# A two-layer network by nested fast products: x's transposes in one burst, stores and weight loads queued behind them, and another order in the first pair

## The chip, the cores and the metric

The kernel runs on one core of one Trainium2 chip. The metric is the device time of one execution in microseconds (us), as a median of several runs. TensorE (PE) multiplies matrices into PSUM banks. VectorE (DVE) and ScalarE (ACT) read those banks and do elementwise work. GpSimd (POOL) and SyncE (SP) mostly issue transfers here. All transfers run on the core's 16 DMA engines. A transfer is issued on the queue of SP, ACT or POOL, and the instructions of one queue are taken in order.

## The reference

`x` is 8 x 1024 x 1024, `w1` 1024 x 4096 and `w2` 4096 x 1024, all float32.

```python
h = x @ w1
h = 0.5 * h * (1 + np.tanh(np.sqrt(2 / np.pi) * (h + 0.044715 * h ** 3)))
return (h @ w2).astype(np.float32)
```

## The kernel before

**Tiling.** The 8192 rows of `x` are taken in eight superblocks of 1024 rows, numbered 0 to 7. In each, both matrix products are split into 2 x 2 blocks, named "11", "12", "21" and "22", and computed by a scheme of seven products instead of eight. Products 1, 2, 3 and 4 use a plain block on the weights' side or on the rows' side, and products 5, 6 and 7 use sums of blocks on both. Superblocks 0 and 1 use the scheme once (`matmul1`, `matmul2_made`). Superblocks 2 to 7 use it twice, one inside the other. They load all sums of the weights from DRAM, where superblocks 0 and 1 have stored them.

**The first layer, in superblocks 0 and 1.** `matmul1` walks over pairs of column chunks (j = 0 to 7). A pair has seven products of two halves each, and 4 matmuls of 128 x 512 for each half (L501), so 56 matmuls. Product 4 of a pair runs at the start of the next pair, after the next pair's product 1. The weights come in groups of four chunks, two pairs to a group (`MadeQuad`). A group holds the four raw blocks of `w1` and the sums 5, 6, 7 and 4 of them. In superblock 1 the raw blocks are loaded from DRAM (L202), the sums are made on VectorE, and each is stored for later superblocks (L247). `inner_sums(m)` makes four further sums of operand m, which only the later superblocks need, in four short VectorE instructions, and stores them (L260). The rows' side is `XOps`: x's four transposed blocks and the sums x5 = 21 + 22, x7 = 11 - 21, x6 = 22 - x7, x3 = x6 - 12.

**The second layer, in superblock 0.** `matmul2_made` runs products 1, 2, 5, 6, 3, 7 and 4 in this order. A plain one has four rows q of 16 matmuls (L1184), so `(6, 3)` is the last row of product 6. Product 3 is "deep": it is itself computed by seven smaller products (L1129, class `Inner`) and has seven steps. After each row or step, `run` carries out the jobs that the table `FILL` lists under that place. Their letters mean: `g`, sums of the activated rows; `wMq`, part q of the sum M of `w2`'s blocks, for product M; `pMN`, the split N of operand M of `w2`, a sum that later superblocks need (it is made on VectorE and stored in `in_d`, L1012); `a`, sums for the deep product; `x`, a sum of x's blocks; `q`, a sum of `w1`'s first group; `i`, inner sums of that group. Product 4 reads all four parts `w40` to `w43`, and its row q goes on in the bank that product 7's row q has used, after VectorE's addition has read that bank.

**x for the next superblock.** After row `(5, 0)` POOL issues eight transfers that cast x's rows to float16 into the DRAM tile `xb` (L476). After row `(6, 3)` SP issues 16 transposing transfers (L165), four for each block, in the order 22, 21, 12, 11. Ahead of them on SP stand twelve stores (`keep`) of `w2`'s blocks 21, 12 and 22, four each. After row `(7, 0)` the first group of `w1` for superblock 1 is loaded on ACT's queue.

**Buffers.** The pool `up` has 24 buffers of 4 KiB per partition (tiles named `u`). They hold `w2`'s blocks and the sums written over them, splits, x's blocks, x's sums and groups of `w1`. The pool `mp` (tiles `mu`) has two; the splits 7 and 4 of operands 1, 2 and 3 are made there. A buffer is free again when its last reader is done, and a store counts as a reader until it has landed. The deep product 3 reads the splits of operand 3 from these tiles.

**Order.** A planner orders each engine's instructions when the kernel is built. What is pinned (`keep_in_program_order`, `load_in_order`, `tt(..., pin=True)`) stays behind the instruction traced before it on its engine. The loads of `MadeQuad` and the stores of the splits are not pinned; all VectorE work named here is.

Of the kernel before, what the change touches and what calls it, by code (L numbers as in the profile page):

```python
# [23 lines left out]
SUMS = tuple(W_SUM)  # L24
# [13 lines left out]
""".split()  # L38
BEGIN = {"m37": (0,), "m24": (1,2), "m34": (3, 4)}
SPLIT_IN_M1 = ()  # L40


def slots(table):
# [6 lines left out]
    ;50:w60 w61;51:w62 w63;52:g30 g31;53:g32 g33  # L50
    ;60:p35 p36;61:a35 p37;62:a37 p34;63:a36
    ;31:w70;32:a33;33:w71;34:w72;35:w73;36:p25;37:p26
    ;70:p27 p24;71:w40 w41;72:w42 w43;73:x5;40:q5;41:x7 x6;42:x3 q6 q7 q4
    ;43:i2 i7 i3 i1 i5""".replace("\n    ", "")),
    slots("""10:g60 w50;11:g61 w51;12:g62 w52;13:g63 w53
    ;20:g50 p55;21:g51 p56;22:g52 p57;23:g53 p54
    ;50:w60 w61;51:w62 w63;52:g30 g31;53:g32 g33
# [18 lines left out]
def kernel(  # L76
# [7 lines left out]
    nc = tc.nc  # L84
# [107 lines left out]
    class MadeQuad:  # L192


        def __init__(self, q, first, store):
            self.q, self.first, self.store = q, first, store
            self.raw = {b: unit(2 * KH, 2 * P) for b in BLOCKS}
            self.ops = {m: self.raw[b] for m, b in W_TERM.items()}
            if not first:
                queue = nc.sync if q else nc.scalar  # L200
                for b in ("12", "11", "22", "21") if q else ("12", "11", "21", "22"):
                    queue.dma_start(out=halves(self.raw[b]), in_=w1_at(q, term.get(b, b)))  # L202

        def load(self):
# [330 lines left out]
    def matmul1(xs, sb, quads, start=None):  # L535
        g = g_tiles()

        def gelu(b, c, src):
            gelu_into(g[b][:, c, :], src)

        def ahead(j):

            if j // 2 == NI // QC - 1:
                return ()
            q, second = divmod(j, 2)
            if not second:
                quad = MadeQuad(q + 1, sb == 0, sb == 1)
                quads.append(quad)
                if sb == 0:
                    quad.load()  # L550
                    quads[q].keep_raw()
            quad = quads[q + 1]
            if sb == 0:
                return [lambda m=m: quad.sum(m, pin=True) for m in SUMS] if second else ()
            jobs = [lambda m=m: quad.sum(m, pin=True) for m in ((7, 4) if second else (5, 6))]
            inner = ((2, 7, 5, 3) if second else (1,)) if q == 0 else ((2, 7, 3) if second else ())
            return jobs + [lambda m=m: quad.inner_sums(m) for m in inner]

        nxt = {}
        splits = []  # L560
        late = None
        for j in range(NI // 2):
            cs = (2 * j, 2 * j + 1)
            end = j == NI // 2 - 1
            source = quads[j // 2]
            if start is not None and j == 0:
                start.pair(gelu)
                ahead(j)
                continue
            jobs = list(ahead(j))  # L570
            banks_a = [psum(), psum()]
            a = [temp(), temp()]

            def one(h):
                product(banks_a[h], source, xs, 1, cs[h], True)
                act_copy(a[h], banks_a[h])

            swap = sb == 1 and j == 0
            for h in range(0 if swap else 2):
                one(h)  # L580
            banks_c, p5, t = [], [], [temp(), temp()]

            def five(h):
                if len(p5) == h:
                    banks_c.append(psum())
                    p5.append(temp())
                    product(banks_c[h], source, xs, 5, cs[h], True)
                    act_copy(p5[h], banks_c[h])

            def six(h):  # L590
                product(banks_a[h], source, xs, 6, cs[h], False)
                act_copy(t[h], banks_a[h])

            def seven(h):
                product(banks_a[h], source, xs, 7, cs[h], False)
                tt(p5[h], banks_a[h], p5[h], SUB, True)

            def three(h):
                product(banks_c[h], source, xs, 3, cs[h], False)

            banks_b = [psum(), psum()]
            for h in range(2):
                if late is not None:
                    gelu("12", late[1][h], late[3][h])
                if late is not None:
                    product(late[2][h], late[0], xs, 4, late[1][h], False)
                    gelu("21", late[1][h], late[2][h])
                elif swap:
                    five(h)
            for h in range(2):  # L610
                product(banks_b[h], source, xs, 2, cs[h], True)
            for h in range(2 if swap else 0):
                one(h)
            for h in range(2):
                add(a[h], banks_b[h])
            difference(g, j - 1)
            half = (len(jobs) + 1) // 2
            if start is not None and j == 1:
                rest = jobs[2:]
                half, jobs = 2, [lambda m=m: quads[0].sum(m, (2, 2), True) for m in (7, 4)] + jobs[:2]  # L620
            elif start is not None and j == 2:
                half, jobs = 2, rest
            if sb == 1:
                half = 3 if j % 2 else 0
                if j != 4:
                    jobs += splits
                    splits = []
            for job in jobs[:half]:
                job()
            if end:  # L630
                six(0)
                gelu("11", cs[0], a[0])
                six(1)
                gelu("11", cs[1], a[1])
                for h in range(2):
                    five(h)
                for h in range(2):
                    seven(h)
                    gelu("22", cs[h], p5[h])
                    three(h)  # L640
                for h in range(2):
                    product(banks_a[h], source, xs, 4, cs[h], False)
                    gelu("21", cs[h], banks_a[h])
                for h in range(2):
                    tt(t[h], t[h], banks_c[h], SUB, True)
                    gelu("12", cs[h], t[h])
            else:
                first = j == 0
                five(0)
                if not first:  # L650
                    gelu("11", cs[0], a[0])
                five(1)
                six(0)
                if not first:
                    gelu("11", cs[1], a[1])
                six(1)
                for h in range(2 if first else 0):
                    gelu("11", cs[h], a[h])
                three(0)
                three(1)  # L660
                seven(0)
                seven(1)
                for h in range(2):
                    gelu("22", cs[h], p5[h])
                for h in range(2):
                    tt(t[h], t[h], banks_c[h], SUB, True)
                late = (source, cs, banks_a, t)
            for job in jobs[half:]:
                job()
            if sb == 1 and j < 2 * len(SPLIT_IN_M1):  # L670
                splits = split_in_m1(SPLIT_IN_M1[j // 2], j % 2)
            if sb == 1 and j > 4:
                for q in {5: (0,), 6: (1,), 7: (2, 3)}[j]:
                    nxt["xb"] = x_cast_paced(sb + 1, g["11"][:, 2 * j + 1, :], 2 * q, nxt.get("xb"))
        difference(g, NI // 2 - 1)
        return g, nxt.get("xb")
# [175 lines left out]
    def matmul2_made(sb, g, keep_w1, xb):  # L852
# [111 lines left out]
        for m, name, first in (  # L964
# [10 lines left out]
            for q in range(NQ):  # L975
# [4 lines left out]
                post(m, q, bank)  # L980
                if (m, q) == (5, 0) and sb == 0:
                    xb = x_cast(sb + 1, nc.gpsimd.tensor_copy(out=pace, in_=p5[0][:, :2]))
                if (m, q) == ((5, 0) if sb else (6, NQ - 1)):
                    xs = XOps(x_transpose(xb, load_in_order))
                if (m, q) == (6, 0):
                    keep("22")
                if (m, q) == (7, 0) and sb == 0:
                    quad = MadeQuad(0, False, True)
# [10 lines left out]
    def split_jobs(m, pieces, t):  # L999

        def operand(v, h):
            if isinstance(v, int):
                return t[v][:, h * QC:(h + 1) * QC, :]
            k, b = int(v[0]) - 1, int(v[1]) - 1
            return chunks(pieces()[2 * k + h])[:, b]

        def make(n):
            u, op, v = W_SUM[n]
            t[n] = (mp.tile([P, NI // 2, OH // 2], DT, name="mu") if n in (7, 4) and m != 4 else unit(NI // 2, OH // 2))
            for h in range(2):  # L1010
                tt(t[n][:, h * QC:(h + 1) * QC, :], operand(u, h), operand(v, h), op, True)
            nc.gpsimd.dma_start(out=in_d[m][:, SUMS.index(n)], in_=t[n])  # L1012

        return [lambda n=n: make(n) for n in SUMS]

# [307 lines left out]
```

## Time and profile before

| | |
|---|---|
| median of 3 runs | 1463.32 us (1462.68 to 1464.65) |
| the profiled execution | 1467.66 us, its span 1465.8 us |
| TensorE busy | 1450.3 us, 99% of the span |
| VectorE busy | 1207.9 us, 82% |
| ScalarE busy | 711.7 us, 49% |
| GpSimd busy | 588.2 us, 40% |
| moved by DMA | 460.13 MB, mean 314 GB/s |
| mean granted TensorE clock | 0.997 |

A line of the timeline gives the start and the length of a merged run of instructions, the engine, the line of the kernel, the operation, what it writes and reads, how many there are, and in brackets how long the engine had been idle before and what released it. `SPq` and `ACTq` are transfers issued on the queues of SP and ACT. A line of the windows gives, for one stretch, its length, each engine's busy time with its count of instructions (PE, PEld, DVE, ACT, POOL), the granted TensorE clock, the busy share of the DMA engines and the GB/s that they moved. A group of transfers shows how long their issue took (least, median, most, in ns), when the first and the last were issued, and the time from issue to landing.

### The profile page before, as it was taken

Reading aid. Unit: us, or ns where it says so; the run is one execution under the profiler, and the core shown is the slowest. Engines: PE = TensorE matmul, PEld = TensorE weight load, DVE = VectorE, ACT = ScalarE, POOL = GpSimd, SP = SyncE. Lnnn points to the kernel's source line nnn. Section 1 sums busy time; section 2 is a strip of 40 time slices with the busy share of each in tenths; the row PEclk is TensorE's granted clock in tenths of the full one; section 3 lists DMA queues with packets and bytes.
Section 4 is the critical chain, followed back from the end, with each engine's and each line's share of the span. In section 5 each row is a group of like instructions: output and inputs, shape, how many; then the busy total and the mean of one; then the engine's idle time right before and its main releaser. Section 6 shows DMA issues by size and latency. Waiting matters only on the chain.

```text
span 1465.8 us, 28916 instructions
## 1 busy us (share of the span) xinstructions
PE 1450.3 (99%) x10731; PEld 1049.1 (72%) x10731; DVE 1207.9 (82%) x2019; ACT 711.7 (49%) x1460; POOL 588.2 (40%) x606
## 2 busy tenths in 40 slices
PE   9999988999999999999999999999999999999998
PEld 5444633444477888778887788777887778877887
DVE  5657748758688898889898898988989889898887
ACT  5665115641158621785228841388224872268621
POOL 1442213222359500793018820388005960068400
PEclk9999999999999999999999999999999999999999
DMA  9999999798799999999999999999999999987594
GB/s 327 336 350 380 330 270 331 256 328 239 275 395 249 287 379 365 330 254 317 352 351 331 241 361 337 366 299 224 386 356 353 264 266 370 354 337 234 207 402 168
DMA packets 199117, 460.13 MB, mean 314 GB/s; under 512 B 75201, under 2 KB 80321, under 8 KB 198081
## 3 DMA queue, kind: packets, MB, share of 16 engines
q1 hardware_dynamic: 176672, 371.25, 74.3%
q0 software_dynamic: 21344, 84.95, 17.9%
q10 hardware_dynamic: 960, 2.10, 0.6%
q8 instruction: 84, 1.38, 0.4%
q14 instruction: 57, 0.46, 0.1%
HBM read 370.15 MB, written 102.76 MB: 323 GB/s over the span
## 4 chain that ended last, share of the span: by engine, by line
PE 85%; DMA 8%; issue 4%; POOL 2%; ACT 1%; SPq 0%; DVE 0%; POOLq 0%; DVEq 0%
PE ps L1129 36%; PE ps L721 23%; PE ps L501 19%; PE ps L1184 6%; DMA gc<-in_w_dram 4%; DMA u<-in_w_dram 2%; DMA w_d<-u 1%; PE ps L434 1%; POOL u L171 1%; DMA xb<-in_x_dram 1%; ACT u L168 0%; POOL in_d L1012 0%; POOL out_dram L838 0%; DMA u<-in_x_dram 0%; PE ps L411 0%
## 5 line engine op out<-in xcount | busy, mean ns | idle before, releaser
L168 ACT COPY tmp<-ps 128x512 f32<-128x512 f32 (+1 forms) x528 | 263.7, 539 | 239.8 <-PE ps L501 155.4
L501 PE MATMUL ps<-u 128*128 128x512 f16 x1472 | 347.1, 382 | 8.7 <-DVE u L141 4.8
L1129 PE MATMUL ps<-u,gc 128*128 128x256 f16 x2704 | 308.6, 273 | 0.0
L1129 PEld LDWEIGHTS <-gc 128*128 128x128 f16 x2816 | 275.5, 98 | 31.9
L141 DVE TENSOR_TENSOR tmp<-tmp,ps 128x256 f32<-128x256 f32 (+1 forms) x368 | 197.1, 543 | 73.6 <-PE ps L721 30.7
L501 PEld LDWEIGHTS <-u 128*128 128x128 f16 x1472 | 144.9, 98 | 153.3 <-issue 9.7
L141 DVE TENSOR_TENSOR u<-u 128x2048 f16<-128x2048 f16 (+3 forms) x292 | 221.2, 801 | 38.4 <-PE ps L1129 14.1
L721 PEld LDWEIGHTS <-u 128*128 128x128 f16 x2096 | 205.0, 98 | 57.3
L850 POOL DMA_DIRECT2D out_dram<-u x50 | 36.7, 735 | 500.6 <-DVE u L141 478.1
L1129 PE MATMUL ps<-u,g 128*128 128x256 f16 x2000 | 234.8, 273 | 0.0
L1129 PEld LDWEIGHTS <-g 128*128 128x128 f16 x2112 | 206.6, 98 | 24.3
L721 PE MATMUL ps<-u 128*128 128x256 f16 x1372 | 221.0, 273 | 0.0
L514 ACT ACTIVATE g<-tmp 128x512 f16<-128x512 f32 x282 | 173.9, 639 | 57.7 <-DVE tmp L141 57.1
L168 ACT COPY ps<-ps 128x256 f32<-128x256 f32 (+1 forms) x208 | 95.2, 458 | 219.5 <-PE ps L1129 219.3
L141 DVE TENSOR_TENSOR ps<-tmp,ps 128x256 f32<-128x256 f32 x444 | 181.4, 426 | 17.1 <-PE ps L721 9.4
L168 ACT COPY u<-ps 128x512 f32<-128x512 f32 (+1 forms) x114 | 66.2, 587 | 179.5 <-PE ps L1129 146.0
L141 DVE TENSOR_TENSOR u<-u,ps 128x512 f32<-128x512 f32 x174 | 118.4, 683 | 40.0 <-ACT u L168 20.0
L514 ACT ACTIVATE g<-ps 128x512 f16<-128x512 f32 x230 | 137.9, 600 | 24.7 <-PE ps L721 14.9
L773 POOL TENSOR_TENSOR tmp<-tmp 128x512 f32<-128x512 f32 x96 | 122.2, 1276 | 41.4 <-DVE tmp L141 31.8
L1184 PE MATMUL ps<-u,g 128*128 128x512 f16 x640 | 138.8, 379 | 0.0
L141 DVE TENSOR_TENSOR tmp<-ps,tmp 128x512 f32<-128x512 f32 x126 | 86.8, 690 | 55.2 <-PE ps L501 46.2
L1184 PEld LDWEIGHTS <-g 128*128 128x128 f16 x640 | 62.6, 98 | 75.3
(72 smaller groups left out, 1571.9 us busy)
## 6 DMA issues: line engine op xcount, KB each, us to landing
u<-w_d SPq DMA_DIRECT2D x343, 512.0 KB, 9.1
u<-in_d SPq DMA_DIRECT2D x162, 512.0 KB, 9.2
out_dram<-u POOLq DMA_DIRECT2D x50, 512.0 KB, 7.6
gc<-in_w_dram SPq DMA_DIRECT2D x48, 512.0 KB, 6.5
g<-w_d SPq DMA_DIRECT2D x45, 512.0 KB, 8.0
w_d<-u POOLq DMA_DIRECT2D x40, 512.0 KB, 6.5
w_d<-u SPq DMA_DIRECT2D x32, 512.0 KB, 9.5
xb<-in_x_dram POOLq DMA_DIRECT2D x56, 256.0 KB, 6.9
```

The lines of the kernel that those rows point to most:

```text
L141: i = nc.vector.tensor_tensor(out=out, in0=in0, in1=in1, op=op)
L168: tc.keep_in_program_order(nc.scalar.copy(out=out, in_=in_))
L171: pool_last[0] = nc.gpsimd.tensor_copy(out=out, in_=in_)
L434: tc.keep_in_program_order(nc.tensor.matmul(bank[:, cols], lhsT=w[:, k, :], rhs=self.xs.blocks[f"{a}{r}"][:, k, cols], start=r == 1 and k ...
L501: tc.keep_in_program_order(nc.tensor.matmul(bank, lhsT=w, rhs=x, start=first and k == 0, stop=k == n - 1, skip_group_check=not first,))
L514: gelu_last[0] = nc.scalar.activation(out=out, in_=src, func=GELU, scale=scale)
L721: tc.keep_in_program_order(nc.tensor.matmul(out, lhsT=w, rhs=x, start=first and k == 0, stop=k == 1, skip_group_check=not first,))
L773: tc.keep_in_program_order(nc.gpsimd.tensor_tensor(out=t, in0=t, in1=temp("p", m), op=ADD))
L850: return nc.gpsimd.dma_start(out=rows, in_=src, **kw)
L1129: tc.keep_in_program_order(nc.tensor.matmul(bank[:, i * OH // 2:(i + 1) * OH // 2], lhsT=t[:, c, i * P:(i + 1) * P], rhs=self.weights(j, c ...
L1184: tc.keep_in_program_order(nc.tensor.matmul(pair(bank), lhsT=a[:, c, :], rhs=chunks(pieces[c // QC])[:, :, c % QC, :], start=(first and c ...
```

## The change

- In superblock 0, the 16 transposes of x for superblock 1 are issued after row `(6, 0)` instead of `(6, 3)`. The four stores of `w2`'s block 22 are issued after `(6, 3)` instead of `(6, 0)`, so behind the transposes.
- The four stores of the splits of operand 3 go to SP's queue instead of POOL's. They are made at the same places as before, which lie behind the transposes in program order.
- The four loads of `w1`'s first group go to SP's queue instead of ACT's, in the order 11, 21, 12, 22 instead of 12, 11, 21, 22.
- The first pair of superblock 1 runs its products in the order 1, 2, 5 like every other pair; before, it ran 5, 2, 1.
- In `FILL[0]`, x7 and x6 come one or two rows earlier, and `q5` moves behind x3. Of five sets of inner sums at `(4, 3)` only set 2 stays. Sets 7 and 3 are made in the first pair, behind its two additions, and sets 1 and 5 in the third (`FIRST_INNER`).

```diff
+FIRST_INNER = {0: (7, 3), 2: (1, 5)}
...
-    ;70:p27 p24;71:w40 w41;72:w42 w43;73:x5;40:q5;41:x7 x6;42:x3 q6 q7 q4
-    ;43:i2 i7 i3 i1 i5""".replace("\n    ", "")),
+    ;70:p27 p24;71:w40 w41;72:w42 w43;73:x5;40:x7;41:x6;42:x3 q5 q6 q7 q4
+    ;43:i2""".replace("\n    ", "")),
...
-                queue = nc.sync if q else nc.scalar
-                for b in ("12", "11", "22", "21") if q else ("12", "11", "21", "22"):
+                queue = nc.sync
+                for b in ("12", "11", "22", "21") if q else ("11", "21", "12", "22"):
...
-            swap = sb == 1 and j == 0
-            for h in range(0 if swap else 2):
+            for h in range(2):
                 one(h)
...
-                elif swap:
-                    five(h)
             for h in range(2):
                 product(banks_b[h], source, xs, 2, cs[h], True)
-            for h in range(2 if swap else 0):
-                one(h)
             for h in range(2):
                 add(a[h], banks_b[h])
...
+            for m in FIRST_INNER.get(j, ()) if sb == 1 else ():
+                quads[0].inner_sums(m)
...
-                if (m, q) == ((5, 0) if sb else (6, NQ - 1)):
+                if (m, q) == ((5, 0) if sb else (6, 0)):
                     xs = XOps(x_transpose(xb, load_in_order))
-                if (m, q) == (6, 0):
+                if (m, q) == (6, 3):
                     keep("22")
...
-            nc.gpsimd.dma_start(out=in_d[m][:, SUMS.index(n)], in_=t[n])
+            (nc.sync if m == 3 else nc.gpsimd).dma_start(out=in_d[m][:, SUMS.index(n)], in_=t[n])
```

## The prediction

> **What bounds the kernel now.** I read the page first, then TensorE's timeline, then every engine's timeline around its gaps, then groups of the DMA queues.
>
> ```profile
> PE 1450.3 (99%) x10731; PEld 1049.1 (72%) x10731; DVE 1207.9 (82%) x2019; ACT 711.7 (49%) x1460; POOL 588.2 (40%) x606
> ```
>
> TensorE is the bound; only its idle and its slow time can be won. Its timeline from 100 to 320 us has two gaps, both between superblocks 0 and 1:
>
> ```profile
> 179.34 27.79 PE L1184 MATMUL ps<-u,g 128*128 128x512 f16 x128
> 211.92 14.70 PE L501 MATMUL ps<-u 128*128 128x512 f16 x56 [4.79 <-DVE u L141]
> 230.56 86.43 PE L501 MATMUL ps<-u 128*128 128x512 f16 x392 [3.94 <-DVE tmp L141]
> ```
>
> Products 7 and 4 end at 207.1; the first pair waits 4.79 us for VectorE, the second 3.94. Windows of 2 us (sixth figure: granted clock) show what follows each gap:
>
> ```profile
> 210.00:212.00 2.00, 0.08 (x1) 0.08 (x2) 1.23 (x1) 0.00 (x0) 0.00 (x0) 0.52 1.11 250
> 212.00:214.00 2.00, 2.00 (x5) 0.64 (x6) 0.00 (x0) 0.15 (x1) 1.23 (x2) 0.50 1.10 315
> 216.00:218.00 2.00, 2.00 (x8) 0.78 (x7) 1.97 (x3) 0.18 (x1) 0.00 (x0) 0.78 1.06 412
> 232.00:234.00 2.00, 2.00 (x6) 0.68 (x5) 1.97 (x3) 2.00 (x5) 0.28 (x1) 0.51 1.00 381
> ```
>
> Half clock costs the first pair 14.70 - 56 x 0.216 = 2.6 us, and the second (3.4 us at half, to 234.9) 1.7. In all 4.8 + 2.6 + 3.9 + 1.7 = 13.0 us can be won. The timeline of all engines says why:
>
> ```profile
> 177.93 27.15 SPq L165 DMA_TRANSPOSE u<-xb  x14
> 200.22 1.23 DVE L141 TENSOR_TENSOR u<-u 128x2048 f16<-128x2048 f16 x1 [6.18 <-DMA u<-xb]
> 201.11 3.66 ACTq L202 DMA_DIRECT2D u<-w_d  x4
> 210.64 1.23 DVE L141 TENSOR_TENSOR u<-u 128x2048 f16<-128x2048 f16 x1 [9.19 <-DMA u<-w_d]
> 214.23 14.48 DVE L141 TENSOR_TENSOR u<-u 128x2048 f16<-128x2048 f16 x26 [2.36 <-DMA u<-xb]
> ```
>
> x5 waits for transposes, q5 for w1's first loads, and 26 sums in a row then hold back the first pair's additions.
>
> **The change part by part.** I follow its order with the times of this trace.
>
> 1. The burst. It needs x's cast rows, and block 22 (transposed first) needs the last ones. The eight casts:
>
> ```profile
> L476 POOL DMA_DIRECT2D xb<-in_x_dram x8: 493/496/527, 149.7 to 153.1; - x8
> DMA to landing us min/median/max: 7.7/10.8/14.0
> ```
>
> The last lands at 153.1 + 14.0 = 167.1. Transposes start at 170.3 today, so passing four stores on SP wins 3.2 us of start, no more; nothing touches the casts. Their pace then is SP's. Today's 16 took 34.8 us, among POOL's stores; eight in a quieter stretch of superblock 2 show:
>
> ```profile
> L165 SPq DMA_TRANSPOSE u<-xb x8: 1122/1252/1622, 649.5 to 659.1; - x8
> DMA to landing us min/median/max: 2.7/3.4/6.3
> ```
>
> (659.1 - 649.5) / 7 = 1.37 us each, so 16 take 21.9: issued by 189.0. I take this row since POOL's four p3 stores leave the stretch, and its later ones wait for VectorE (step 2); the ends are 16 x 1.25 = 20.0 and today's 34.8. The Trainium skill (DMA: Bandwidth & Descriptors, Latency and other measured facts) gives a DMA transpose 261 GB/s: 2.1 MB would take an estimated 8 us, the stores behind would land by about 180, step 2 would cost nothing, and the sum would be the first rival's. The trace's 131 KB per 1.37 us is 96 GB/s and disagrees.
>
> 2. What stands behind the burst: p35, p36, p37, p34, w2's four blocks, w1's four loads. POOL loses four issues of 0.53 us and ACT the 3.66 us of loads at 201.1; neither is on the path (product 4's copies had until 211.9), so 0. The second group's loads now stand behind all this on SP (today issued from 205 to 215), but its sums run at 232. What counts is that landing frees buffers. In deep product 3 the 24 u buffers are all taken: w2's blocks with the sums written over them 16, product 6's halves 2, p35 and p36 2, x's blocks 4. So p25 and p26 need buffers that a store releases, p27 and p24 the two mu buffers of p37 and p34. Today these stores landed at 169 to 176 and VectorE ran:
>
> ```profile
> 179.18 1.28 DVE L141 TENSOR_TENSOR u<-u 128x1024 f16<-128x1024 f16 x2
> 183.67 2.49 DVE L141 TENSOR_TENSOR mu<-u 128x1024 f16<-128x1024 f16 x4
> 187.06 2.35 DVE L141 TENSOR_TENSOR u<-u 128x2048 f16<-128x2048 f16 x2
> 190.51 2.35 DVE L141 TENSOR_TENSOR u<-u 128x2048 f16<-128x2048 f16 x2
> ```
>
> Now p35's store is issued at 189 and lands some 4 us on (2.7 to 6.3 above), at 193; the others 1.45 us apart (512 KB at the 364 GB/s of 226 to 231). VectorE stands from 179.2 to 193. Behind p25 it has, at this trace's starts, put 0.6, p26 1.2, product 7's first addition 0.6, p27 1.2, p24 1.2, the second addition 0.6, w40 1.1; with p25's 1.2 that is 7.7, so w40 is ready at 200.7, w41 at 201.9, and behind one more addition w42 at 203.6 and w43 at 204.8. Product 4 could start at 193.2 (179.34 + 64 x 0.217) but reads all four. TensorE so idles 7.5 us, and runs some 6 us at half clock as after 211.92: row 0's 16 matmuls end at about 207.1, the other 48 (10.4 us) at 217.5. That is 10.4 us later than today. Cover against this would be the stores ahead of the burst; bound from below: 0.
>
> 3. Order 1, 2, 5 and the weights' new queue and order. The first pair needs x's blocks 11 and 12 (landed by 193) and w1's 11, then 21; x5 and q5 3.5 us later, q6 5.2 us later. VectorE is through with the last addition at 205.4, x5, x7, x6, x3 (4 x 1.14) by 210. From 190 the DMA engines owe 12 transfers on SP (17.4 us) and about 11 us of POOL's stores: w1's 22 lands near 219 at 360 GB/s. It is needed by 217.5 + 5.2 - 1.1 = 221.6. Cover 2.6 us: cost 0. By the 234 GB/s of 187 to 207 the debt takes 45 us, 22 lands at 235 and costs 13; I take the fast end, since those windows held transposes and this stretch holds none.
>
> 4. The four inner sums moved. Ahead of the additions VectorE now has one set (1.4 us) for five. Sums 7 and 3 (2.8 us) fall between the additions and product 7's subtraction, which TensorE reaches 10.4 us into the pair: hidden, as are 1 and 5 in the third pair, by the same 10 us. Both second losses (3.9 and 1.7) go.
>
> Sum: the first pair runs from 217.5 for 56 x 0.216 = 12.1, to 229.6. Today the second is free at 230.56 and loses 1.7 more: 232.3. Gain 2.7, of which I leave 0.5 for VectorE's additions: 2.2 us. The profiled execution took 1467.66 (span 1465.8), 4.3 above the median; 2.2 off the median of 1463.32 is 1461.1. By step 1's ends: a burst over at 187 gives 1459, one over at 202 1474; eight transposes among stores (341.8 to 352.2) took 1.48 each, 191 and 1463, so the slow end is left outside the main case.
>
> **Rivals.** *No stall* (the p3 stores pass the burst, not being pinned as the transposes are, so the change does less than it says): product 4 ends at 207.1, w1's 11 lands at 211, as today's q5 at 210.64 shows for the same bytes, and the pair ends at 223.1: 9.2 us won, 1454, or 1457 with 2.6 of half clock. For it: p35 is written by 160, well before 167.1. Against it: p37 and p34 come later, and the burst stands first in program order. *Weights late*, the side that is slower: they stand last, behind eight stores that ACT's queue let them pass. For it, 234 GB/s; against it, 371 from 218 to 226. Each us beyond 221.6 costs one; it decides against the change from 221.6 + 2.2 + 2.9 = 226.7 on; half way between the two landings, 227, it costs 5.4: 1466.5. The Trainium skill (the same page, Issuing engines are not separate DMA queues) says that all issuers share the same 16 engines, so a new queue takes no bytes off; the share near 1.0 in every window agrees. *A buffer of w2's fourth block for p25*: four stores on, 5.8 us later, 1467.
>
> **How the numbers follow.** Main case 0.48, no stall 0.21, weights late 0.21, fourth block's buffer 0.10. About 0.2% (2.9 us) is what this measurement can tell from no change. The main case, 1461.1 with its own range 1456 to 1465, splits 0.16 faster, 0.31 same, 0.01 slower; with the first rival faster, the last two slower: faster 0.37, same 0.31, slower 0.32. The range reaches to 1453 (no stall) and 1469 (weights at 229.5).
>
> **What would show it.** Right: transposes from 167 to 190 on SP; VectorE idle some 14 us from 179 with a DMA named; TensorE idle before product 4, none at 207 and 227. Wrong: VectorE running on at 179 (no stall); transposes beginning later than 170 or among stores; TensorE waiting at the first pair (weights).

## The result and the profile after

The change takes 1466.89 us as a median of 22 runs (1464.70 to 1469.30); the kernel before, run beside it, takes 1463.82 (22 runs, 1460.14 to 1468.27). The ratio is 1.0023 with a 95% interval of 1.0016 to 1.0029: some 3 us slower, where the forecast was 2 us faster. A second comparison later gave 1466.10 against 1464.08, ratio 1.0008 (0.9996 to 1.0020), so the loss is small, but it is no gain. The profiled execution of the change took 1467.82 us, its span is 1466.0. That of before took 1467.66. By these two profiles alone the change would do nothing, and this turns out to be the heart of the case.

The page after, the line of the engines:

```profile
PE 1449.4 (99%) x10731; PEld 1049.3 (72%) x10731; DVE 1207.9 (82%) x2019; ACT 712.2 (49%) x1460; POOL 587.4 (40%) x602
```

TensorE's timeline of the change between 176 and 320 us:

```profile
179.45 13.98 PE L1182 MATMUL ps<-u,g 128*128 128x512 f16 x64
202.13 16.55 PE L1182 MATMUL ps<-u,g 128*128 128x512 f16 x64 [8.70 <-DVE u L142]
218.52 36.59 PE L502 MATMUL ps<-u 128*128 128x512 f16 x168
255.40 60.59 PE L502 MATMUL ps<-u 128*128 128x512 f16 x280 [0.29 <-DVE tmp L142]
315.83 4.48 PE L1182 MATMUL ps<-u,g 128*128 128x512 f16 x20
```

Products 7 and 4, one unbroken run of 128 matmuls before, are cut in two: TensorE stands 8.70 us ahead of product 4, and product 4 takes 16.55 us where product 7 takes 13.98. The two old gaps, ahead of the first and the second pair, are gone. Superblock 1's second layer (last line) begins at 315.83; in the profile of before it began at 316.83.

Windows of the change (sixth figure: granted clock) show why product 4 is slow:

```profile
192.00:194.00 2.00, 1.43 (x7) 0.56 (x6) 0.00 (x0) 0.00 (x0) 0.00 (x0) 1.00 0.93 348
198.00:200.00 2.00, 0.00 (x0) 0.00 (x0) 2.00 (x4) 0.00 (x0) 1.28 (x3) 0.50 1.05 375
204.00:206.00 2.00, 2.00 (x6) 0.66 (x5) 2.00 (x3) 0.00 (x0) 0.55 (x1) 0.50 1.03 393
208.00:210.00 2.00, 2.00 (x11) 0.92 (x10) 1.97 (x2) 0.59 (x1) 0.54 (x1) 1.00 1.02 385
```

The clock falls to 0.50 within the gap (by 198) and stays there for the first 5 us of product 4: 6 matmuls in 2 us instead of 11.

SP's queue and then VectorE, in the timeline of the change:

```profile
168.44 22.73 SPq L166 DMA_TRANSPOSE u<-xb  x16
191.27 1.00 SPq L1010 DMA_DIRECT2D in_d<-u  x2
192.36 2.08 SPq L1010 DMA_DIRECT2D in_d<-mu  x2
194.48 5.42 SPq L166 DMA_DIRECT2D w_d<-u  x4
200.08 16.93 SPq L203 DMA_DIRECT2D u<-w_d  x8
```

```profile
194.24 1.29 DVE L142 TENSOR_TENSOR u<-u 128x1024 f16<-128x1024 f16 x2 [14.87 <-DMA in_d<-u]
219.72 6.27 DVE L142 TENSOR_TENSOR u<-u 128x2048 f16<-128x2048 f16 x8 [8.13 <-DMA u<-w_d]
```

The burst is unbroken. The first store behind it is issued at 191.27, and VectorE, which wants that store's buffer for p25, stands 14.87 us until it has landed. The second line is q5, which now waits for w1's loads at the end of SP's queue; TensorE did not notice.

### The profile page after: what moved, and what is told of

Read it like the earlier page. It is cut to its first block, busy times and chain, and to the rows that moved or that the text cites. A ratio compares the mean times of both kernels' runs of the same rounds, so it can differ in the third digit from the quotient of the medians.

```text
span 1466.0 us, 28909 instructions
## 1 busy us (share of the span) xinstructions
PE 1449.4 (99%) x10731; PEld 1049.3 (72%) x10731; DVE 1207.9 (82%) x2019; ACT 712.2 (49%) x1460; POOL 587.4 (40%) x602
## 4 chain that ended last, share of the span: by engine, by line
PE 96%; SPq 1%; DMA 1%; DVE 1%; issue 0%; ACT 0%; DVEq 0%
PE ps L1127 36%; PE ps L502 26%; PE ps L719 23%; PE ps L1182 11%; SPq L166 1%; PE ps L435 1%; DMA u<-in_d 1%; DVE u L142 0%; DMA u<-in_x_dram 0%; PE ps L412 0%; DMA in_d<-u 0%; DVE mu L142 0%; ACT u L169 0%; DVE tmp L142 0%; PE ps L370 0%
## 5 line engine op out<-in xcount | busy, mean ns | idle before, releaser
L502 PE MATMUL ps<-u 128*128 128x512 f16 x1472 | 343.2, 379 | 0.3 <-DVE tmp L142 0.3
L142 DVE TENSOR_TENSOR tmp<-tmp,ps 128x256 f32<-128x256 f32 (+1 forms) x368 | 197.1, 544 | 71.5 <-PE ps L719 30.6
```

The costliest lines, as they stand in the source:

```text
L142: i = nc.vector.tensor_tensor(out=out, in0=in0, in1=in1, op=op)
L502: tc.keep_in_program_order(nc.tensor.matmul(bank, lhsT=w, rhs=x, start=first and k == 0, stop=k == n - 1, skip_group_check=not first,))
```

## The experiments

All times are medians in us (12 executions of each edited kernel, 9 of e2, 6 of e4); each comparison ran beside the kernel before (1463.8 to 1464.1 in all of them). "Second layer" is the start of superblock 1's second layer in TensorE's timeline.

| kernel | time | ratio to before (95%) | second layer at |
|---|---|---|---|
| before, profile shown / two more | 1467.66 / 1467.33, 1463.15 (one each) | | 316.83 / 315.68, 312.24 |
| the change, profile shown / again | 1466.89 / 1466.10 | 1.0023 (1.0016 to 1.0029) / 1.0008 (0.9996 to 1.0020) | 315.83 / 313.86 |
| e1: splits' stores on POOL | 1467.94 | 1.0022 (1.0012 to 1.0031) | 317.19 |
| e2: burst ahead of block 22's stores, alone | 1467.71 | 1.0022 (1.0009 to 1.0034) | 317.91 |
| e3: order and moved sums, alone | 1463.38 | 0.9996 (0.9985 to 1.0006) | 310.79 |
| e4: block 22's stores ahead | 1470.44 | 1.0048 (1.0033 to 1.0064) | 316.79 |
| e5 / e8: no store behind the burst | 1461.32 / 1459.80 | 0.9981 (0.9967 to 0.9994) / 0.9970 (0.9956 to 0.9984) | 308.17 / 306.10 |
| e6: both groups of stores on POOL | 1468.64 | 1.0014 (0.9988 to 1.0040) | 322.02 (the longest of its executions) |
| e7: burst cut in two | 1468.08 | 1.0032 (1.0015 to 1.0049) | 315.17 |
| e9: w1's first loads on SP, alone | 1463.31 | 0.9993 (0.9981 to 1.0005) | 310.62 |

### The baseline: before again, twice

The kernel of before, unedited.

> The kernel before, unchanged, profiled a second time. Its first profiled execution took 1467.66 us, 3.8 above the median of 22 runs (1463.82); the change's took 1467.82, only 0.9 above its own (1466.89). If the losses between superblocks 0 and 1 are always those of the first profile, this shows gaps of some 4.8 and 3.9 us on TensorE again (8.7 together). If the kernel before varies there, and the first profile was a long one, an execution near 1463.8 us shows some 4 us less of gaps and half clock.

> The kernel before once more, for a third profile. Theory (the sum failed by its baseline: the profiled execution of before was one of its long ones, and a usual one loses less at the two gaps): an execution near 1463 shows less than 13.0 us in the two gaps and the half clock behind them, by about as much as it is shorter than 1467.66. Rival (executions differ elsewhere, not at the gaps): the two gaps and the half clock are again 12 to 14 us whatever the execution's time.

The first repeat took 1467.33, another long one: gaps of 1.95, 1.91 and 4.31 us between 207 and 230 and two stretches of half clock behind them (1.7 and 1.8 us lost), 11.7 in all. The second took 1463.15, the kernel's median. TensorE's timeline of that one:

```profile
207.28 5.34 PE L501 MATMUL ps<-u 128*128 128x512 f16 x24
214.57 7.08 PE L501 MATMUL ps<-u 128*128 128x512 f16 x32 [1.95 <-DVE u L141]
225.95 86.45 PE L501 MATMUL ps<-u 128*128 128x512 f16 x392 [4.30 <-DVE tmp L141]
312.24 7.93 PE L1184 MATMUL ps<-u,g 128*128 128x512 f16 x36
```

In this execution the first gap is 1.95 us instead of 4.79, and the clock stays full behind it:

```profile
214.00:216.00 2.00, 1.43 (x7) 0.70 (x8) 2.00 (x3) 0.36 (x1) 1.19 (x3) 1.00 0.94 364
228.00:230.00 2.00, 2.00 (x6) 0.72 (x5) 1.97 (x2) 2.00 (x5) 0.67 (x1) 0.50 0.85 324
```

Only the second gap costs half clock: 86.45 - 392 x 0.216 = 1.8. In all 1.95 + 4.30 + 1.8 = 8.0 us can be won, not 13.0. The execution is 4.51 shorter than the one in the prediction, and its second layer begins 4.59 earlier. From there to the end (time less start) the three executions of before are alike: 1150.8, 1151.7 and 1150.9. So the difference lies ahead of the second layer. How it differs can be read on the queues: in this execution ACT issued w1's loads at 198.78 instead of 201.11, the last transposes went at 201.0 instead of 203.8, and q5 began at 205.72 instead of 210.64. Why the queues ran ahead in this execution is not shown.

An estimate says the same of the other executions: with 1150.8 to 1151.7 us from there to the end, one that takes the median of 1463.82 begins its second layer at 312.1 to 313.0, near this one and not near 316.83. The clocks of the timed executions fit, though they do not say where an execution lost its time. Of 85 of the kernel before, 28 had a mean clock of 0.999 (1463.3 on average), 40 of 0.998 (1464.6) and 17 of 0.997 (1466.3). The profile that the prediction used had 0.997. Of the change's 34, none had 0.999.

### The change again

> The change once more, timed beside the kernel before and the next two. 1465 to 1468 by its first median of 1466.89. Theory (its loss is set by queue order and so is the same in every execution): TensorE's gap ahead of product 4 is 8 to 12 us again with 9 to 12 us of half clock behind it. Rival (the gap is a chance of that execution): under 5 us.

1466.10. Its profiled execution took 1464.89, with the same gap, somewhat smaller (TensorE's timeline, then VectorE's):

```profile
199.64 16.23 PE L1182 MATMUL ps<-u,g 128*128 128x512 f16 x64 [5.85 <-DVE u L142]
313.86 6.42 PE L1182 MATMUL ps<-u,g 128*128 128x512 f16 x29
```

```profile
191.75 1.29 DVE L142 TENSOR_TENSOR u<-u 128x1024 f16<-128x1024 f16 x2 [12.03 <-DMA in_d<-u]
```

The gap fell below the 8 to 12 us that the expectation named, since SP began the burst at 166.62 here, 1.8 earlier, and took 1.2 less for it. But it is there, with the same releaser. Half clock behind it costs 16.23 - 13.98 (product 7's time for as many matmuls) = 2.3 us, so it lasts some 4.5 us, and not the 9 to 12 that were expected. VectorE's stand belongs to the kernel, not to one execution.

### Which store holds VectorE

e1 takes the change and gives the stores of operand 3's splits back to POOL:

```diff
-            (nc.sync if m == 3 else nc.gpsimd).dma_start(out=in_d[m][:, SUMS.index(n)], in_=t[n])
+            nc.gpsimd.dma_start(out=in_d[m][:, SUMS.index(n)], in_=t[n])
```

> The change, but with the four p3 stores on POOL's queue again. Theory (buffers): VectorE stood from 179.4 to 194.2 us because p25 to p24 need the buffers of p35 to p34, whose stores stood behind the burst. Then VectorE runs on at 179, the 8.7 us gap before product 4 is gone, TensorE waits 2 to 6 us for w1's first block at 207, and the time is 1456 to 1460 us. Rival (bytes): the DMA engines owe the same bytes whoever issues them, so w1's blocks land at 217 to 221 as in the change; then the gap moves from 193 to 207 with about its length, and the time stays at 1465 to 1468.

1467.94: not faster at all. TensorE's timeline, and VectorE's:

```profile
203.83 16.83 PE L1182 MATMUL ps<-u,g 128*128 128x512 f16 x64 [10.28 <-DVE u L142]
```

```profile
197.75 1.29 DVE L142 TENSOR_TENSOR u<-u 128x1024 f16<-128x1024 f16 x2 [16.44 <-DMA w_d<-u]
```

The gap is where it was, and VectorE stands 16.44 us, but now for `w_d<-u`, a store of w2's fourth block. p25 finds the buffer of a split that POOL has stored, and runs at 179.42; p26 wants one of block 22, whose stores are still behind the burst. The theory had the right mechanism and the wrong set of stores. The rival, a gap that comes back at the first pair because as many bytes are owed, did not come either.

e2 takes the kernel before and makes only the swap of the burst and block 22's stores:

```diff
-                if (m, q) == ((5, 0) if sb else (6, NQ - 1)):
+                if (m, q) == ((5, 0) if sb else (6, 0)):
                     xs = XOps(x_transpose(xb, load_in_order))
-                if (m, q) == (6, 0):
+                if (m, q) == (6, 3):
                     keep("22")
```

> The kernel before with the burst after row (6, 0) and w2's block 22 stored after (6, 3), and nothing else of the change. Theory (buffers): moving the burst does no harm; x5 no longer waits, product 4 ends at 207, q5 has its blocks by about 207 to 210, and of the second gap 1 to 4 us stay since the 26 sums still stand ahead of the first pair's additions: 1454 to 1460 us. Rival (bytes): the first gap stays at 4 to 5 us and so does the second: 1462 to 1465.

1467.71, outside both expected ranges. TensorE's timeline, and VectorE's:

```profile
206.00 15.39 PE L1184 MATMUL ps<-u,g 128*128 128x512 f16 x64 [11.83 <-DVE u L141]
```

```profile
199.91 1.29 DVE L141 TENSOR_TENSOR u<-u 128x1024 f16<-128x1024 f16 x2 [18.00 <-DMA w_d<-u]
```

The swap alone makes a loss as large as that of the whole change. VectorE's stand, again for block 22's stores, was in neither the theory nor the rival.

e4 is the other half: the change with block 22's stores ahead of the burst again, the splits' stores still behind it.

```diff
+                if (m, q) == (6, 0):
+                    keep("22")
                 if (m, q) == ((5, 0) if sb else (6, 0)):
                     xs = XOps(x_transpose(xb, load_in_order))
-                if (m, q) == (6, 3):
-                    keep("22")
```

> The change, but with the four stores of w2's fourth block ahead of the burst on SP again; the stores of operand 3's splits stay behind it. Theory (VectorE stands as long as any store that holds a buffer it needs next is queued behind the 16 transposes, whichever store that is): the burst starts near 171 instead of 168 and ends at 193 to 203, the first split's store lands some 3 us later, so VectorE stands until 196 to 206, TensorE idles 10 to 19 us ahead of product 4, and the time is 1466 to 1476. Rival (the fourth block's stores alone are at fault): VectorE does not stand, no gap ahead of product 4, 1459 to 1464.

1470.44, as the theory said and not the rival. TensorE's timeline, and VectorE's:

```profile
204.88 15.39 PE L1182 MATMUL ps<-u,g 128*128 128x512 f16 x64 [11.33 <-DVE u L142]
```

```profile
196.99 1.29 DVE L142 TENSOR_TENSOR u<-u 128x1024 f16<-128x1024 f16 x2 [17.50 <-DMA in_d<-u]
```

Either group of stores behind the burst is enough to hold VectorE. So it takes both ahead of it, or on another queue, to know what the rest of the change is worth. e5, and e8 as its repeat, do that: block 22's stores as in e4, the splits' stores as in e1, everything else as the change.

> As e4_22_ahead, and the stores of operand 3's splits issued by POOL again, so no store stands behind the burst. Theory: VectorE does not stand near 180, TensorE goes from product 7 into product 4 without a gap, and waits 2 to 5 us for the last transposes at the end of product 4, as in e3_order_alone; 1460 to 1465. Rival (w1's loads on SP, behind everything, are what costs): the gap at the first pair is over 6 us with the loads named, 1466 or more. Against e3_order_alone the two differ only in the queue of w1's first four loads.

> The kernel of e5_22_ahead_p3_pool again: the fourth block's stores ahead of the burst, the splits' stores on POOL, everything else as the change. Theory: again faster than the kernel before, 1459 to 1463, and 4 to 7 us faster than the change on the same chip; TensorE's gaps between 179 and 250 us add to less than 5 us. Rival (its first lead was chance): within 0.1% of the kernel before.

1461.32, then 1459.80, where the change took 1466.10 in the same comparison: 6.3 us less. This version beats both kernels: against before its ratio is 0.9970 (0.9956 to 0.9984). TensorE's timeline of e8:

```profile
179.38 27.79 PE L1182 MATMUL ps<-u,g 128*128 128x512 f16 x128
207.01 3.62 PE L502 MATMUL ps<-u 128*128 128x512 f16 x16
211.17 8.81 PE L502 MATMUL ps<-u 128*128 128x512 f16 x40 [0.55 <-DVE u L142]
221.01 24.33 PE L502 MATMUL ps<-u 128*128 128x512 f16 x112 [1.03 <-DVE tmp L142]
245.66 60.59 PE L502 MATMUL ps<-u 128*128 128x512 f16 x280 [0.32 <-DVE tmp L142]
306.10 14.19 PE L1182 MATMUL ps<-u,g 128*128 128x512 f16 x65
497.48 5.60 PE L1127 MATMUL ps<-u,gc 128*128 128x256 f16 x48 [1.52 <-DMA u<-in_d]
```

Products 7 and 4 are one run again, three gaps between 207 and 246 add to 1.9 us, and the clock stays full there (16 matmuls take 3.62 us and 40 take 8.81, 0.22 each). The second layer begins 6.1 us ahead of the 1463.15 us execution of before. Not all of it is kept: at 496 TensorE waits 1.52 us for a load of operand splits, where that execution of before has no gap, and e8's profiled execution (1458.64) is 4.5 shorter. In e5's the same wait is 4.04 us, with half clock behind it: an execution of 1465.80, although its second layer began at 308.17. In these two executions TensorE came earlier and met the next transfer that was late. The wait of 2 to 5 us for the last transposes, which e5's expectation named, did not come: no gap of e5 between 180 and 250 is over 1.02.

### What the other parts are worth alone

e3 is the kernel before with the order 1, 2, 5, the moved inner sums and the new order of w1's loads, still on ACT; burst and stores as before (the diff is that of the change without the lines on `nc.sync`, `x_transpose` and `keep`).

> The kernel before with the order 1, 2, 5 of the first pair, the moved sums and the new order of w1's blocks (still on ACT's queue), but with the burst, block 22's stores and the p3 stores where they were. Both theories: the first pair starts when x's block 11, transposed last, has landed (214.1 in the first profile), so the first gap is 6 to 7 us; the second gap is gone, since one set of inner sums instead of five stands ahead of the additions: 1458 to 1462 us. If it is not faster than the kernel before, the sums were not what held the second gap.

1463.38, no change, and longer than the 1458 to 1462 expected. TensorE's timeline:

```profile
210.84 2.97 PE L502 MATMUL ps<-u 128*128 128x512 f16 x13 [2.38 <-DMA u<-xb]
215.86 95.10 PE L502 MATMUL ps<-u 128*128 128x512 f16 x432 [2.05 <-DVE u L142]
```

The second gap of before (4.30) is gone, as step 4 said. The first is 2.38 + 2.05, against 1.95 in the execution of 1463.15, since the new order starts with product 1 and so with x's block 11, which is transposed last. ACT's loads of w1, issued from 197.8 to 201.3, were on the engines together with the last transposes.

e9 is the kernel before with only the queue changed:

```diff
-                queue = nc.sync if q else nc.scalar
+                queue = nc.sync
```

> The kernel before, and one part of the change alone: w1's first four loads on SP behind the transposes, in before's order, in place of ACT's queue. Theory (loads that ACT issues between the transposes land ahead of the last of them and delay them; behind the burst they can't): the last transposes land some 5 us earlier than 210, but q5, made from w1's 22 and 12, waits for loads that come later, so the two about balance: 1461 to 1465. Rival (loads late): the first gap at 207 grows to 8 us or more, 1466 to 1469.

1463.31, no change that can be told. TensorE's timeline:

```profile
208.17 12.26 PE L501 MATMUL ps<-u 128*128 128x512 f16 x56 [0.34 <-DVE u L141]
224.33 86.45 PE L501 MATMUL ps<-u 128*128 128x512 f16 x392 [3.91 <-DVE tmp L141]
```

Here the first gap goes and the second stays. SP issued the last transpose at 199.7, against 201.0 and 203.8 in two executions of before. Loads that stand behind the burst cannot get between its transfers. Each of the two parts takes away one of the two gaps, and they need each other: e8, which has both, gains 4.3 us, while e3 and e9 gain 0.5 and 0.8, less than their intervals. In e5 and e8 the burst also stands earlier in the program than in e3, but behind the same twelve stores it starts at about the same time: at 171.56 and 169.96, against 171.05 in e3 and 169.52 in e9.

### A burst among other transfers

e6 leaves the burst where the change has it and puts both groups of stores on POOL:

```diff
-                    load_in_order(w2_at(q, term.get(b, b)), raw[b][q])
+                    if b == "22":
+                        tc.keep_in_program_order(nc.gpsimd.dma_start(out=w2_at(q, term.get(b, b)), in_=raw[b][q]))
+                    else:
+                        load_in_order(w2_at(q, term.get(b, b)), raw[b][q])
...
-            (nc.sync if m == 3 else nc.gpsimd).dma_start(out=in_d[m][:, SUMS.index(n)], in_=t[n])
+            nc.gpsimd.dma_start(out=in_d[m][:, SUMS.index(n)], in_=t[n])
```

> The change with both groups of stores on POOL, so that the burst of 16 goes from near 168 to 190 on SP as in the change, and nothing but w1's loads stands behind it. Theory: VectorE is not held by a store behind transposes, no gap ahead of product 4; the last transposes land by 195, w1's loads from 198 to 212, so a gap of 0 to 4 us at 207; 1457 to 1462. Rival (the transposes themselves, by the share they take of the transfer engines, delay the stores and with them VectorE): VectorE stands 5 us or more, 1463 to 1467.

Neither. Of twelve executions five took 1457.9 to 1461.0, as the theory said, and seven 1468.5 to 1475.2. The profile is of the longest. Its SP queue, and TensorE:

```profile
168.49 48.95 SPq L166 DMA_TRANSPOSE u<-xb  x16
```

```profile
222.50 39.67 PE L502 MATMUL ps<-u 128*128 128x512 f16 x170 [13.88 <-DMA u<-w_d]
```

VectorE is not held at 180, and products 7 and 4 run through. But the burst takes 48.95 us instead of 22.73, w1's loads behind it come after 217, and TensorE stands 13.88 us ahead of the first pair. Windows of e6 and then of the change, within their bursts (the last two figures are the DMA engines' share and GB/s):

```profile
176.00:186.00 10.00, 10.00 (x70) 6.67 (x69) 8.70 (x13) 0.00 (x0) 2.60 (x4) 1.00 1.11 230
186.00:196.00 10.00, 10.00 (x48) 4.57 (x47) 8.63 (x11) 0.00 (x0) 2.16 (x4) 1.00 1.26 140
```

```profile
168.00:180.00 12.00, 12.00 (x110) 10.55 (x108) 10.27 (x12) 1.14 (x2) 0.33 (x1) 1.00 0.54 118
180.00:190.00 10.00, 10.00 (x48) 4.51 (x46) 0.00 (x0) 0.00 (x0) 0.43 (x1) 1.00 0.67 144
```

Between the stores a transpose takes 10.8 us from issue to landing (median) against 2.9 in the change, and POOL's stores of 512 KB take 16 to 18. From 186 to 196 the engines are wholly busy and move 140 GB/s. In the change their share within the burst is only 0.54 and 0.67, and POOL's timeline shows two reasons. From 153.9 to 179.67 POOL issues nothing: the stores that it issues from 160.69 to 172.13 in e6 stand behind the burst on SP here. From 179.4 on VectorE stands, and POOL's next store of a split waits 15.41 us for it, until 195.84. So the second half of the change's quick burst is bought with the very stand that makes it slow. Two other profiles fit this: the burst takes 27.41 us in e1, where the splits' stores are on POOL and VectorE stands, and 32.37 in e8, where it does not stand. Why five executions escape this is open; no profile fell on one.

e7 cuts the burst: blocks 12 and 11 first, then block 22's stores, then blocks 22 and 21; the rest as e3.

```diff
-                if (m, q) == ((5, 0) if sb else (6, NQ - 1)):
-                    xs = XOps(x_transpose(xb, load_in_order))
-                if (m, q) == (6, 0):
+                if sb == 0 and (m, q) == (6, 0):
+                    xs = XOps(x_transpose(xb, load_in_order, which=(2, 3)))
+                if sb == 0 and (m, q) == (6, NQ - 1):
                     keep("22")
+                    x_transpose(xb, load_in_order, xs.blocks, (0, 1))
+                if sb and (m, q) == (5, 0):
+                    xs = XOps(x_transpose(xb, load_in_order))
```

> The new order of the pairs and the moved sums, w1's loads on ACT, the splits' stores on POOL; the burst is cut in two: blocks 12 and 11, whose rows are cast first, after product 6's first row, then the four stores of w2's fourth block, then blocks 22 and 21. Theory: the first eight transposes run from about 162 to 175 while the fourth block is still being made, its stores land by 182 before VectorE needs their buffers, the other eight end near 192, and neither the gap ahead of product 4 nor the one at the first pair is over 1 us: 1456 to 1460. Rival (VectorE stands for the stores, now 3 to 6 us later than in the kernel before): a gap of 2 to 5 us ahead of product 4 with the clock at half behind it, 1461 to 1466.

1468.08. VectorE's timeline, and TensorE's:

```profile
188.63 1.29 DVE L142 TENSOR_TENSOR u<-u 128x1024 f16<-128x1024 f16 x2 [6.87 <-DMA w_d<-u]
```

```profile
194.72 2.16 PE L1185 MATMUL ps<-u,g 128*128 128x512 f16 x8 [0.70 <-DVE u L142]
219.17 43.07 PE L502 MATMUL ps<-u 128*128 128x512 f16 x186 [5.61 <-DVE u L142]
```

The first eight transposes, among the stores of the splits, took 19.8 us from 163.5 on instead of the expected 13. So block 22's stores were late, VectorE stood 6.87 us (the rival's mechanism), and the last eight delayed the first pair (VectorE waits 13.70 us for `u<-xb`, until 212.97), which neither had said.

## Why the prediction was wrong

**The step that failed is the sum, by its baseline.** "Gain 2.7 ... 2.2 off the median of 1463.32" set the forecast for the changed kernel against "232.3 today", the time in one execution of 1467.66 at which the second pair is free, with its half clock added, and then took the difference off a median 4.3 us lower. The text noted the 4.3 and did not ask where they lay. They lay in the 13.0 us that it called winnable. In the execution of 1463.15 the same point lies at 225.95 + 1.8 = 227.7, and the forecast's own 229.6, with the 0.5 it left, is 2.4 us later: 1465.7, which is slower, and within 1.2 us of the 1466.89 measured. That execution is one profile; that it is the usual one is supported by its time, by the estimate of 312.1 to 313.0 for a median execution and by the clocks of the 85 timed executions, not by more timelines.

**What the change does was forecast nearly as it came.** From 229.6 + 0.5 and today's 84.5 us from the pair to the second layer, that layer should have begun at 314.6; it began at 315.83 and 313.86.

- Step 1, the burst. 16 transposes in 21.9 us, issued by 189.0: measured 22.73 and 191.2, in the repeat 21.53 and 188.2. The Trainium skill (DMA: Bandwidth & Descriptors, Latency and other measured facts) has 261 GB/s for DMA transposes, measured on one kernel with a non-contiguous middle dimension; the trace disagrees, 2.1 MB in 22.73 us are 92 GB/s here.
- Step 2, the stand. VectorE from 179.2 to 193, TensorE idle 7.5 us, product 4 ending at 217.5: measured 179.4 to 194.24, 8.70 us and 218.5; in the repeat 191.75, 5.85 and 215.7. The 10.4 us it should cost product 4 are 11.4 and 8.3. Half clock cost 2.6 and 2.3 us where 3 were put. "Cover against this would be the stores ahead of the burst" was right, and e1 and e4 against e5 show that neither group of four stores may stand behind it.
- Step 3, the weights. Cost 0 held: no gap in the first pair. That the loads behind the burst also free its last transfers was missed; e9 shows the first gap at 0.34 by that alone.
- Step 4, the inner sums. The second loss went: 4.30 to nothing at that place, and 0.29 at 255. The text let the half clock behind it last 3.4 us "to 234.9"; from 230.56 that is 234.0, and its cost of 1.7 stands.

**The rivals.** No stall did not come: all five kernels with a store behind the burst had VectorE standing, four of them for 12 us and more in every profile (e7, cut in two, for 6.87). Weights late did not come. The buffer of w2's fourth block was not what p25 waited for, but it is the next in line: e1 shows p26 waiting for it when the first cause is taken away. The range, 1453 to 1469, held the time. The 1466.5 and 1467 of the last two rivals lie next to it by luck, since neither thing happened.

## What to carry to other kernels

When the profiled execution is longer than the median, look for the surplus in the stage that you mean to improve before you set a gain against it; profile the kernel before a second and third time if its executions differ. A store that must land before a buffer is free belongs ahead of any long group of transfers on its queue, and moving one of two such groups showed nothing here, because the other took its place. Another queue is not always a way out: e6, with all eight stores on POOL, lost in seven of twelve executions. Two edits that each remove one gap of two may only pay together.

## What the hardware showed beyond this

Transposing transfers and ordinary stores in flight together slowed each other: 48.95 us for 16 transposes in e6 against 21.5 to 22.7 in the change, at a full share of the DMA engines and with 140 GB/s moved from 186 to 196, where the change moved 382 from 194 to 210, without transposes. In that execution the overlap won nothing: POOL's queue moved 8.45 MB from 168 to 218 in e6, an estimated 22 us at 382 GB/s, and with the transposes of the change that makes 44 to 45 us one after the other. The same kernel also ran without that loss in five of twelve executions.

Half clock did not follow from the length of a gap alone. In the execution of before that took 1463.15, 1.95 us of idle were followed by full clock, 32 matmuls in 7.08 us. In the one that took 1467.33, a gap of the same length at 207 was followed by half clock (TensorE's timeline of that one):

```profile
209.05 7.04 PE L501 MATMUL ps<-u 128*128 128x512 f16 x24 [1.95 <-DVE u L141]
218.00 7.08 PE L501 MATMUL ps<-u 128*128 128x512 f16 x32 [1.91 <-DVE u L141]
```

24 matmuls took as long as 32 did after the next gap. With each of the 13 gaps of 3.9 us and more in these profiles the clock fell to 0.50, but 2.4 to 5.4 us after the idle had begun: at 197.1 in the change, 3.7 us into its gap, at 196.0 in e1, 2.4 us into its gap, and at 225.6 in e9, 1.3 us after its gap of 3.91 was over.
